# A 128-byte shift of the left-hand tile pools in a one-core decoder trunk

## The chip, the cores and the metric

The kernel runs on one core of a Trainium2 chip. The metric is the time of one execution on the device in microseconds (us). The kernel before took 1058.08 us, the median of three runs.

## The reference

A two-layer decoder trunk over 256 tokens of width 1024, in float32. Each layer is a half-step SwiGLU feed-forward, a token mixer (RWKV-7 time mixing in the first layer, banded attention in the second) and a second half-step feed-forward, each inside a pair of RMS norms. The four feed-forwards hold most of the work:

```python
D_MODEL, SEQ, D_FF = 1024, 256, 2816
def swiglu(x, w_in, w_out):
    gate, up = jnp.split(x @ w_in, 2, axis=-1)
    return (jax.nn.silu(gate) * up) @ w_out

for layer in range(DEPTH):                       # DEPTH = 2
    g = norm_g[layer]
    h = h + 0.5 * rms_norm(swiglu(rms_norm(h, g[0]), ffn_w_in[layer, 0], ffn_w_out[layer, 0]), g[1])
    u = rms_norm(h, g[2])
    m = rwkv7_time_mix(u, ...) if layer < 1 else swa_sinks(u, k_sh, v_sh, ...)
    h = h + rms_norm(m, g[3])
    h = h + 0.5 * rms_norm(swiglu(rms_norm(h, g[4]), ffn_w_in[layer, 1], ffn_w_out[layer, 1]), g[5])
```

After the first layer a shared key and value is projected from the normed residual.

## The kernel before

**Products.** A float32 product is made from float32r halves: each operand is split into a high part (a cast) and the rest (`stream`, L165, for weights; `split`, L313, for activations). `mm3` (L226) then makes three matmuls, high by high, high by low, low by high. The first operand of a matmul is the stationary one, which a weight load (PEld) brings into the array; the second is the moving one, read while the matmul runs.

**Weights.** All weights are streamed in chunks of 128 x 1024 float32 (512 KB). A chunk lands in a staging tile `wr` (L161), ScalarE casts it into the high half of a weight tile (L195), and VectorE subtracts to get the low half (L201). Weight tiles are 8 KB per partition, and come in three pools, `W1`, `W2`, `W3`, in turns:

```python
self.turns = ["W1", "W2", "W2", "W1", "W2", "W2", "W1", "W2"]            # L1483, first feed-forward
self.turns, self.wturn = ["W3"] * 4 + ["W1"] * 3 + ["W2"] * 4, 0         # L1205, the other three and attention
```

The profile leaves out buffer numbers and prints all three as `W`; which pool a chunk lies in follows from counting chunks along `turns`, as the program's allocation does.

**The feed-forward.** `ffn_main` (L449) goes over blocks `b` of 256 hidden features. For each, `feat_pair` (L354) makes the up-projection: the weight is stationary and the normed activations `xt` are moving, in pairs of a 512-column (L362) and a 256-column matmul (L363), 8 pairs for each of the four chunks of `w_in` that a block takes, so 32 pairs a block. Then `down` (L436) makes the down-projection of an earlier block: here the gated activations `g2k` are stationary and the weight is moving, 24 matmuls of 512 columns a block in `mm3` (L227), 12 for each chunk of `w_out`. The last blocks' down-projections run together after the loop (`ffn_tail`, L480; in the third feed-forward `t_end` in the attention region): 72 matmuls in the first feed-forward, 96 in the others. The profile's group `bk<-W,g2k` of L227 is exactly these, 1056 of them, 88 chunks.

Three smaller groups run through L227: the first blocks of each feed-forward, projections of queries, and others with `xt` stationary (`bk<-W,xtl`, `bk<-W,xth`); the shared key and value and the attention's output projection with tiles of pool `ux` stationary (`bk<-W,u`, `bk<-W,xx`); and the time mixer's output projection (`bk<-wo,BK`).

**Where tiles lie.** Each partition's memory is filled by pools from both ends. From the left come the permanent tiles, then `xt`, then a small spacer pool (`sh0`, `sh1` or `sh2`, one for each of the three regions of the program), and then, in the first and third region, the left-hand pools: `W1` (three weight tiles), `g2k` (14 tiles for gated activations and products), `t4` (tiles of 128 x 1024 for norms), and in the third region also `qT`, and `kvp` with the kept key and value. From the right come `ux`, `W2`, `W3` and in the second region the mixer's tiles. Tile sizes in the left-hand pools are multiples of 256 bytes, so that all tiles behind the spacer lie at the same address modulo 256 (their residue below). `xt` begins at residue 0, the spacer is 24 x 4 = 96 bytes, and so `W1`, `g2k`, `t4`, `qT` and `kvp` lie at 96. The right-hand end of the usable memory is at residue 224, and so `W2`, `W3` and `ux` lie at 224. The staging tiles `wr` lie at 64, the identity matrix at 128. Of the second region `sh1` is not touched; most tiles there lie at 224 behind one tile of 8320 bytes, and those of `wo0` and `wo3` at 96.

Order: the program's instructions are put in order by the tile framework, by data and by hand-written lists (`STEPS`, `ATT`) in the second region and the attention. All weight loads are issued by SyncE in one queue.

Of the kernel before, what the change touches and what calls it, by code (L numbers as in the profile page):

```python
# [16 lines left out]
P = 128  # L17
# [60 lines left out]
class Trunk:  # L78
# [508 lines left out]
    def tm_core(self):  # L587
# [35 lines left out]

        acc0, todo = v_half(0, xv)
        run(todo)
        self.mix(xkm[:, :, toks[1]], 2, toks[1])
        self.tm_lora(1)
# [564 lines left out]
        self.close("el1", "Wx", "GR", "GS", "el", "sh1", "xt", "ar")  # L1192
        self.open("xt")
        self.open("sh2")
        self.tl("sh2", [P, 24])
        self.open("g2k", 14)
        self.open("W1", 3)
        self.open("qT")
# [271 lines left out]
    def run(self, out):  # L1470
        nc, a = self.nc, self.a
        self.out = out
        self.tm_open()
        self.open("xt")
        self.open("sh0")
        self.tl("sh0", [P, 24])
        self.open("W1", 3)
        self.open("t4", 4)
        self.open("g2k", 14)
        self.tm_begin()  # L1480
        self.open("l1", side="right")
        self.open("W2", 5, side="right")
        self.turns = ["W1", "W2", "W2", "W1", "W2", "W2", "W1", "W2"]  # L1483

        self.ffn_begin(0, None, 2, 3)
        g_pre = self.gain(R_NORM[(0, 0)])
        self.lead_chunk(0, 0)
        nc.sync.dma_start(self.h[1], a["x"][P:T, :])
        self.xt = xt = self.new_xt("xt")
        for i in range(2):  # L1490
            self.to_xt(i, self.hstat(i), [(g_pre, xt)])
        self.ffn_lead((0, 1))
        self.ffn_main()
        self.load(self.cols, a["cols"], self.mid)
        self.load(self.small, a["small"].to_broadcast([P, 272]), self.mid)
        self.load(self.cst[:, P:], a["consts"][:, P:], self.mid)
        self.tm_consts()
        g_post = self.gain(R_NORM[(0, 1)], self.mid)
        for i in range(2):
            self.tm_in(i, self.post(i, self.ffn_tail(i), g_post, True))  # L1500
        accs, g_post = self.tm_core()

        g_pre = self.gain(R_NORM[(0, 4)])
        xt = self.new_xt("xt")
        for i in range(2):
            self.to_xt(i, self.post(i, accs[i], g_post, False), [(g_pre, xt)])
        self.ffn_begin(1, xt)
        self.plan = list(P1)
        for i in range(2):
            self.ffn_lead((i,))  # L1510
        self.ffn_main()
        g_post = self.gain(R_NORM[(0, 5)], self.mid)

        self.kv_open()
        xt = self.new_xt("xt")
        xe = self.new_xt("ux", ("u", "xx"))
        self.plan = list(PKV)
        self.wkv = [self.stream(a["w_kv"][c], gains=C_GKV + 2 * c) for c in range(3)]
        for i in range(2):
            self.to_xt2(i, self.post(i, self.ffn_tail(i, self.early(i, TX1)), g_post, True), xe, xt)  # L1520
        self.ffn_begin(2, xt, 1)
        for i in range(2):
            self.kv(i, xe)
            self.ffn_lead((i,))
        self.ffn_main()
        self.att_region()
        self.ffn_main()
        g_post = self.gain(R_NORM[(1, 5)], self.mid)
        for i in range(2):
            self.post_last(i, self.ffn_tail(i), g_post)  # L1530
        for p in reversed(self.psum):
            p.release()
        self.close("W3", "W2", "ux", "kvp", "t4", "pad", "qT", "W1", "g2k", "sh2", "xt")
# [88 lines left out]
```

## Time and profile before

| | |
|---|---|
| median of three runs | 1058.08 us (1057.75 to 1059.89) |
| the profiled execution | 1058.52 us, of which the span is 1056.7 us |
| TensorE busy (PE) | 1027.6 us, 97% of the span, 6264 matmuls |
| VectorE busy (DVE) | 699.5 us, 66% |
| ScalarE busy (ACT) | 565.3 us, 53% |
| mean traffic of the memory | 172 GB/s over the span |

The page's first part gives the busy time of each engine, the second the same in 40 slices of the span, the fourth the chain of work that ended last. The time of a single matmul is modelled at its end, and matmuls overlap in the array: the duration of a 512-column matmul reads some 390 ns where the next one begins some 230 ns later. So lengths of whole runs of matmuls are read from the chain in order of time, where pieces stand one behind the other, and the durations serve to compare matmuls of one shape.

### The profile page before, as it was taken

What the parts mean: (1) busy time and instruction counts of PE and PEld (TensorE: products, weight loads), DVE (VectorE), ACT (ScalarE), POOL (GpSimd) and SP (SyncE); (2) the same over time, 40 slices, a digit from 0 to 9 for tenths busy, and PEclk for the clock granted to TensorE, in tenths of its full rate; (3) what the DMA queues carried; (4) which work ended last, traced back from release to release, by engine and by line L of the source; (5) the groups of instructions that cost most, each with busy time, mean ns of one, the idle gap of its engine ahead of it and who ended that gap; (6) DMA issues with size and microseconds to landing.
All of it is one profiled execution on the core that took longest, in us unless ns stands there. A gap on an engine that the chain in (4) does not pass through costs nothing.

```text
span 1056.7 us, 16152 instructions
## 1 busy us (share of the span) xinstructions
PE 1027.6 (97%) x6264; PEld 859.3 (81%) x6264; DVE 699.5 (66%) x1125; ACT 565.3 (53%) x1014; POOL 20.5 (2%) x34
## 2 busy tenths in 40 slices
PE   6999999999999999999999999999999979999997
PEld 5888888779967887888888788888877758888885
DVE  6766655527798977766665676666658876765652
ACT  6654554355244546655455665455556755655541
POOL 0000000000000001000000000000010000000000
PEclk9999999999999999999999999999999999999999
DMA  8868665034354346766563376675535127766621
GB/s 285 248 187 279 220 193 165 23 117 141 120 167 135 122 134 207 258 199 206 194 182 122 116 268 212 209 237 189 180 104 175 41 94 254 237 214 196 183 78 40
DMA packets 52668, 183.04 MB, mean 173 GB/s; under 512 B 5744, under 2 KB 6000, under 8 KB 52464
## 3 DMA queue, kind: packets, MB, share of 16 engines
q1 hardware_dynamic: 52304, 181.49, 53.4%
q8 instruction: 49, 0.80, 0.3%
q10 hardware_dynamic: 288, 0.52, 0.1%
q14 instruction: 27, 0.22, 0.1%
HBM read 180.94 MB, written 1.05 MB: 172 GB/s over the span
## 4 chain that ended last, share of the span: by engine, by line
PE 91%; ACT 3%; DVE 3%; DMA 1%; issue 1%; POOL 0%; SPq 0%; DVEq 0%; POOLq 0%; ACTq 0%
PE bk L227 36%; PE bt L362 13%; PE bk L362 13%; PE bt L363 7%; PE bk L363 7%; PE bk L571 3%; PE bk L617 2%; PE bk L581 1%; PE bt L309 1%; PE bc L1002 1%; PE bk L1053 1%; ACT W L195 1%; PE bk L1397 1%; ACT g2k L1368 1%; DVE t L259 0%
## 5 line engine op out<-in xcount | busy, mean ns | idle before, releaser
L201 DVE TENSOR_TENSOR W<-wr,W 128x1024 fp32r<-128x1024 f32 x280 | 341.2, 1225 | 192.8 <-ACT W L195 191.9
L195 ACT CAST W<-wr 128x1024 fp32r<-128x1024 f32 x280 | 291.8, 1050 | 190.7 <-issue 96.5
L227 PE MATMUL bk<-W,g2k 128*128 128x512 f32 x1056 | 250.7, 394 | 0.0
L227 PEld LDWEIGHTS bk<-W,g2k 128*128 128x128 f32 x1056 | 196.1, 188 | 44.1
L362 PE MATMUL bk<-xtl,W 128*128 128x512 f32 x296 | 104.8, 392 | 0.0
L362 PE MATMUL bt<-xth,W 128*128 128x512 f32 x296 | 104.6, 391 | 0.0
L362 PE MATMUL bt<-xtl,W 128*128 128x512 f32 x296 | 104.4, 391 | 0.0
L362 PE MATMUL bk<-xth,W 128*128 128x512 f32 x296 | 104.4, 391 | 0.0
L363 PE MATMUL bt<-xth,W 128*128 128x256 f32 x296 | 83.3, 281 | 0.0
L363 PE MATMUL bk<-xth,W 128*128 128x256 f32 x296 | 83.2, 281 | 0.0
L363 PE MATMUL bk<-xtl,W 128*128 128x256 f32 x296 | 83.2, 281 | 0.0
L363 PE MATMUL bt<-xtl,W 128*128 128x256 f32 x296 | 83.1, 281 | 0.0
L227 PE MATMUL bk<-W,xtl 128*128 128x512 f32 x216 | 60.4, 427 | 6.4 <-ACT W L195 3.5
L362 PEld LDWEIGHTS bt<-xtl,W 128*128 128x128 f32 x296 | 55.6, 188 | 12.3 <-DVE xtl L350 0.5
L362 PEld LDWEIGHTS bk<-xtl,W 128*128 128x128 f32 x296 | 55.6, 188 | 12.2
L362 PEld LDWEIGHTS bk<-xth,W 128*128 128x128 f32 x296 | 55.6, 188 | 11.9
L362 PEld LDWEIGHTS bt<-xth,W 128*128 128x128 f32 x296 | 55.5, 188 | 11.8
L227 PEld LDWEIGHTS bk<-W,xtl 128*128 128x128 f32 x216 | 42.0, 200 | 20.0 <-ACT W L195 4.0
L363 PEld LDWEIGHTS bk<-xtl,W 128*128 128x128 f32 x296 | 55.9, 189 | 1.4
L363 PEld LDWEIGHTS bt<-xth,W 128*128 128x128 f32 x296 | 55.8, 189 | 0.1
L363 PEld LDWEIGHTS bt<-xtl,W 128*128 128x128 f32 x296 | 55.8, 189 | 0.1
L363 PEld LDWEIGHTS bk<-xth,W 128*128 128x128 f32 x296 | 55.8, 189 | 0.0
(287 smaller groups left out, 1375.7 us busy)
## 6 DMA issues: line engine op xcount, KB each, us to landing
wr<-in_w_in_dram SPq DMA_DIRECT2D x148, 512.0 KB, 3.8
wr<-in_w_out_dram SPq DMA_DIRECT2D x88, 512.0 KB, 3.6
wr<-in_w_in_lead_dram SPq DMA_DIRECT2D x28, 512.0 KB, 4.2
wr<-in_w_v_dram SPq DMA_DIRECT2D x16, 512.0 KB, 3.9
gain<-in_rows_dram SPq DMA_DIRECT2D x13, 512.0 KB, 4.5
wr<-in_w_k_dram SPq DMA_DIRECT2D x8, 512.0 KB, 4.0
wr<-in_w_r_dram SPq DMA_DIRECT2D x8, 512.0 KB, 3.5
wr<-in_w_o_dram SPq DMA_DIRECT2D x8, 512.0 KB, 4.3
```

The lines of the kernel that those rows point to most:

```text
L195: self.follow(nc.scalar.copy(w[:, 0, :], raw), 0)
L201: self.follow(nc.vector.tensor_tensor(w[:, 1, :], raw, w[:, 0, :], op=ALU.subtract), 1)
L227: mm = lambda *x, **y: self.nc.tensor.matmul(*x, **y, **kw)
L309: t = self.nc.tensor.transpose(b[:, k * P:(k + 1) * P], xn[:, c:c + P], self.ident)
L362: mm(banks[j], hi[:, c0:c0 + P], xt[c][:, :, k4, :], start=(k == 0), stop=False)
L363: use[0] = mm(banks[j][:, 0:T], lo[:, c0:c0 + P], xt[c][:, 0, k4, :], start=False, stop=(k == KT - 1))
L571: self.nc.tensor.matmul(b[:, j * T:(j + 1) * T], ws[k // 4][:, c0:c0 + P], xf[:, k, :], start=(k == 0), stop=(k == KT - 1))
L581: nc.tensor.matmul(bs[j], l[:, k, j * P:(j + 1) * P], x[:, k, sl], start=(k == 0 and not e), stop=(k == KT - 1 and e == 1))
L617: mm(acc, x[:, 2 * k2 + k, :], w[:, k, :], start=(k2 + k == 0), stop=(k2 + k == 4))
L1002: mm(b[r, m * N:(m + 1) * N], W[r, v - hh * 16, :], XV[r, v, :], start=True, stop=True)
L1053: mm(out[hh][half[1 - e], m * N:(m + 1) * N], lhs, UV[part][:, hh * 16 + q, :], start=(not i and part == 0 and m == 0), stop=(part == e), ...
L1368: nc.scalar.activation(S[x], S[x], AF.Exp, bias=st[:, 1, x:x + 1], accum_out=st[:, 3, x:x + 1])
```

## The change

Two spacer tiles grow from 24 to 56 float32 numbers, from 96 to 224 bytes:

```diff
@@ tm_core, where the third region opens @@
         self.open("xt")
         self.open("sh2")
-        self.tl("sh2", [P, 24])
+        self.tl("sh2", [P, 56])
         self.open("g2k", 14)
         self.open("W1", 3)
@@ run, where the first region opens @@
         self.open("xt")
         self.open("sh0")
-        self.tl("sh0", [P, 24])
+        self.tl("sh0", [P, 56])
         self.open("W1", 3)
```

Nothing is ever written to or read from a spacer. Every tile behind it on the left moves by 128 bytes. 322 of the program's 1061 tiles move:

| tiles | residue modulo 256 before | after |
|---|---|---|
| `W1`, `g2k`, `t4`, `qT`, `kvp` | 96 | 224 |
| `W2`, `W3`, `ux` | 224 | 224 |
| `xt` | 0 | 0 |
| `wr` | 64 | 64 |
| identity matrix | 128 | 128 |
| second region (`sh1` and what lies behind it) | 96 or 224 | the same |

The instructions of the program, their order on each engine and their waits are the same before and after, row for row, on TensorE, VectorE, ScalarE, GpSimd and SyncE. Only addresses differ.

## Rows read from the trace of the kernel before

**Rows 1.** The page: busy time of three engines, and slices.

```profile
PE 1027.6 (97%) x6264; PEld 859.3 (81%) x6264; DVE 699.5 (66%) x1125; ACT 565.3 (53%) x1014; POOL 20.5 (2%) x34
...
PE   6999999999999999999999999999999979999997
...
PEclk9999999999999999999999999999999999999999
```

**Rows 2.** The page: chain that ended last, share of the span by engine, line.

```profile
PE 91%; ACT 3%; DVE 3%; DMA 1%; issue 1%; POOL 0%; SPq 0%; DVEq 0%; POOLq 0%; ACTq 0%
PE bk L227 36%; PE bt L362 13%; PE bk L362 13%; PE bt L363 7%; PE bk L363 7%; PE bk L571 3%; PE bk L617 2%; PE bk L581 1%; PE bt L309 1%; PE bc L1002 1%; PE bk L1053 1%; ACT W L195 1%; PE bk L1397 1%; ACT g2k L1368 1%; DVE t L259 0%
```

**Rows 3.** Busy time in two stretches, one block long each: start:end, length, engines, clock.

```profile
655.90:672.50 16.60, 16.60 (x90) 14.22 (x89) 10.14 (x16) 8.83 (x14) 0.00 (x0) 1.00 0.63 192
...
705.90:722.50 16.60, 16.60 (x90) 14.28 (x89) 10.13 (x15) 8.82 (x14) 0.00 (x0) 1.00 0.61 189
```

**Rows 4.** Chain in order of time, third feed-forward: start us, us, what, matmuls.

```profile
655.95 5.57 PE bk L227 x24
672.63 5.58 PE bk L227 x24
689.30 5.50 PE bk L227 x24
705.92 5.58 PE bk L227 x24
722.59 5.46 PE bk L227 x24
```

**Rows 5.** Chain in order of time: first feed-forward's blocks and tail; last tail.

```profile
47.99 5.60 PE bk L227 x24
64.72 5.51 PE bk L227 x24
81.35 5.53 PE bk L227 x24
...
181.28 16.05 PE bk L227 x69
...
1027.87 22.26 PE bk L227 x96
```

**Rows 6.** Line L227, all: count, duration ns min/median/max, first and last start.

```profile
L227 PE MATMUL bk<-W,g2k x1056: 387/393/483, 47.8 to 1049.7; 128*128 128x512 f32 x176
...
L227 PE MATMUL bk<-W,xtl x216: 388/396/796, 9.7 to 891.1; 128*128 128x512 f32 x108
...
L227 PE MATMUL bk<-wo,BK x96: 387/389/498, 372.9 to 395.6; 128*128 128x512 f32 x96
...
L227 PE MATMUL bk<-W,u x72: 387/392/504, 586.0 to 848.6; 128*128 128x512 f32 x72
```

**Rows 7.** Line L227 in two stretches, key and value at 588.9, attention output at 828.2.

```profile
L227 PE MATMUL bk<-W,xx x12: 388/389/389, 589.0 to 591.5; 128*128 128x512 f32 x12
...
L227 PE MATMUL bk<-W,xx x12: 392/395/398, 829.7 to 832.3; 128*128 128x512 f32 x12
```

**Rows 8.** Lines L195 and L201, all weight splits: duration ns min/median/max.

```profile
L195 ACT CAST W<-wr x280: 1027/1049/1075, 8.1 to 1019.6; 128x1024 fp32r<-128x1024 f32 x140
...
L201 DVE TENSOR_TENSOR W<-wr,W x280: 1183/1225/1229, 9.2 to 1020.7; 128x1024 fp32r<-128x1024 f32 x140
```

**Rows 9.** Transposes of two lines, matmuls: duration ns min/median/max.

```profile
L806 PE MATMUL bc<-cst,p x16: 272/273/273, 253.6 to 281.3; 128*128 128x128 f32 x16
...
L431 PE MATMUL bk<-cst,g2k x22: 270/272/273, 35.8 to 899.8; 128*128 128x128 f32 x22
```

**Rows 10.** What PE waited for, longest first: us in total, times, longest.

```profile
PE bt L309 <- DVE t L301: 7.7, 1, 7.7
PE bk L227 <- ACT W L195: 3.5, 2, 1.8
PE bk L581 <- ACT u L543: 1.6, 2, 1.4
```

## The prediction

> **What bounds the kernel now.** The page's busy times come first [rows 1]: TensorE is busy 97% of the span, no slice after the first falls under 0.7, and its clock is granted in full throughout, the higher of its two levels, 2.4 GHz. The chain of work that ended last says the same [rows 2]: 91% of it is TensorE's, 36% line L227 alone and 40% the up-projection's lines L362 and L363. TensorE's three longest waits add up to 12.8 us [rows 10]. A stretch of one regular block of a feed-forward, 16.60 us long, has TensorE busy for all of it, VectorE for 10.1 us and ScalarE for 8.8 us, with DMA at 0.6 [rows 3]: the engines that split the weights have 6 us to spare in each block. So here a nanosecond less in a matmul is a nanosecond less in the time, and nothing but matmuls matters much. The change moves no instruction, so the only question is whether a matmul, or what feeds it, takes another time when its operands lie elsewhere.
>
> **What the trace shows of addresses.** The kernel before holds both cases side by side, since W1 lies at residue 96 with g2k, and W2 and W3 at 224. The down-projection of one block is 24 matmuls on two chunks, g2k stationary and W moving. Counted along `turns`, the five blocks of [rows 4] use two W3 chunks (5.57 us), two W2 (5.58), a W3 and a W1 (5.50), two W2 (5.58) and two W1 (5.46). In the first feed-forward two W2 chunks take 5.60 us, one W2 and one W1 5.51 or 5.53 [rows 5]. There the instructions, shapes and surroundings are the same. Where both chunks share the residue of g2k the block takes 0.12 us less than where neither does, and with one of them it lies between: 0.06 us a chunk of 12 matmuls, 5 ns a matmul.
>
> That it is the agreement of the two operands, and not the left side or the number 96, shows where 224 meets 224. `wo` by BK, 72 of 96 with both at 224, has a median of 389 ns, against 393 for W by g2k, of which 74% disagree, and 396 for W by xtl, all of which disagree, with xt at 0 [rows 6]. In the key and value projection W3 moves against xx, both at 224: twelve matmuls between 388 and 389 ns. In the attention's output projection W1, at 96, moves against the same xx: twelve between 392 and 395 at the median, up to 398 [rows 7]. One row speaks less clearly: W by u has 392 ns at the median, though 60 of its 72 agree [rows 6]; they stand at the beginnings of runs, where matmuls still wait for data.
>
> **The change part by part.**
>
> *Down-projections.* 1056 matmuls are 88 chunks. 23 of them lie in W1 and agree already; 65 lie in W2 or W3 and will agree. At 0.06 us each that is 65 x 0.06 = 3.9 us off. In the tails, where W1 chunks alternate with others, they don't reach their 5.46 us a block: the last one takes 22.26 us for 96 matmuls [rows 5] where four blocks of 5.46 would be 21.84, 0.42 less, while its five W2 and W3 chunks alone account for 0.30. This adds 0.1 in each of the two tails that are so mixed, 0.2 in all. From below: if the settled runs of two like chunks are special and only 3 ns a matmul come, 65 x 12 x 3 ns = 2.3 us.
>
> *W1 against u and xx.* 36 matmuls disagree now (96 against 224) and will agree; at 395 against 389 ns [rows 7] that is 0.2 us off.
>
> *W1 against xt.* 168 matmuls go from 96 against 0 to 224 against 0. They disagree before and after, so nothing is taken; up to 0.2 us either way (1 ns each).
>
> *Up-projections.* Here W is stationary and xt, at 0, moves. Between the blocks of [rows 4] stand stretches of 32 pairs: 661.52 to 672.63 is 11.11 us with three W1 chunks and one other, 11.09 with no W1, 11.12 with two, 11.09 with none. W1 costs 0.01 us a chunk at most. If that is its residue, moving its 45 up-projection chunks to 224 gives back 0.4 us; if it is that W1 shares its residue with g2k, which is being written then, all 103 chunks of W2 and W3 will pay it, 1.0 us more. I take 0, between them.
>
> *Splits, norms, transposes.* The casts of weights run from 1027 to 1075 ns with a median of 1049, the subtractions from 1183 to 1229 [rows 8], although 85 of the 280 write to residue 96 and 195 to 224: there are no two levels, and what moves costs nothing. Should they cost 5% more, the 6 us a block that VectorE has to spare hide it. Transposes against the identity at 128 take 272 ns with the tile at 96 (g2k, L431) and 273 with it at 224 (p, L806) [rows 9]: nothing. Scores and values of the attention have both operands in pools that move together.
>
> *Sum.* 3.9 + 0.2 + 0.2 = 4.3 us. These matmuls stand on the chain as whole runs [rows 4, 5], and the weights' loads wait for tiles that TensorE frees, so they begin earlier by as much; of TensorE's 3.5 us of waiting for a weight split [rows 10] a little may grow. I take 0.1 off: 4.2 us. Against the profiled execution's 1058.5 us this gives 1054.3. The median of the runs shown is 0.4 lower; that goes into the range.
>
> **The Trainium skill, weighed against this.** The Trainium skill's page "SBUF — State Buffer" says in its section "SBUF: two separate sides" that within the engines' side only the port pair shared by VectorE and GpSimd contends, and in "A bandwidth-pool intuition that's wrong (but worth ruling out)" that TensorE's weight loads have a read port of their own. By that rule the place of g2k and W can't matter to a matmul, the sum would be 0 and the time 1058.5 us. The trace disagrees by the 0.12 us between like blocks [rows 4], and the measurement decides; the rule's result is the second rival.
>
> **The rivals.**
>
> *Part of the gain.* The agreement helps, but after the change ScalarE and VectorE also write at the residue that TensorE reads, everywhere. Then only the lower 2.3 us come, and the up-projections pay their 1.0: 1058.5 - 1.3 = 1057.2 us. For it: W1's 0.01 us a chunk. Against it: W1 and g2k share a residue already, with g2k written all the time, and that is where the block is shortest.
>
> *No effect.* The 5 ns belong to something that goes with W1, such as its neighbours in time, and not to residues. Then 1058.5 us. Against it stand 224 by 224 at 389 ns and W1 by xx at 395 [rows 6, 7].
>
> *Slower.* In the up-projections W2 and W3, stationary at 224, are loaded while g2k is written; today g2k lies at 96. If the new agreement of writes with weight loads costs these matmuls what disagreement costs the others, 5 ns on each of the 2368 of L362 and L363, that is 11.8 us: 1058.5 - 4.2 + 11.8 = 1066.1 us. From 2.7 ns a matmul (6.3 us) the kernel would be slower by over 0.2%. Against it: the three W1 chunks at 661.52, which agree with g2k today, add 0.02 us in 11.11 us, 0.4 ns for each of their 48 matmuls.
>
> **How the numbers follow.** The forecast has 0.73, between 3.3 and 5.0 us off. Part of the gain has 0.11, no effect 0.10, slower 0.06. A measurement of this kernel can tell about 0.2% (2.1 us) from no change. All of the forecast's case is faster by more, and about a third of the partial one: 0.76. No effect and the rest of the partial case are the same: 0.18. Slower has 0.06. The range goes from 1053.2 (the whole sum with the 0.4 of the up-projections, against the lower median) to 1057.4 (the partial case), which leaves out no effect, slower and a little at the edges.
>
> **What would show it.** Right: the down-projection blocks of 24 matmuls all at 5.45 to 5.48 us on the chain, whichever pool they use; the last tail near 21.9; the median of W by g2k at 389 ns, equal to that of `wo` by BK; up-projection stretches still at 11.09 to 11.12; blocks 16.55 us apart where they are 16.6 to 16.7 now. Wrong: blocks with W2 or W3 still at 5.58 (no effect), or up-projection stretches over 11.2 us (the slower rival), or TensorE waiting longer for splits (L195, L201) by as much as the matmuls gain.

## The result and the profile after

The changed kernel takes 1053.16 us, the median of five runs (1051.64 to 1054.67), against 1058.08 us; the ratio is 0.9949, 95% interval 0.9932 to 0.9967. That is 4.9 us less, where 4.2 were forecast, and the time is 0.04 us under the low end of the forecast's range. The profiled execution is the slowest of the five (1054.67 us): its span is 1052.9 us, 3.8 less than the profiled execution before.

The chain of the changed kernel in order of time (start us, us, what, matmuls), against [rows 4, 5]:

```profile
48.32 5.45 PE bk L227 x24
64.88 5.45 PE bk L227 x24
...
180.85 15.67 PE bk L227 x69
...
653.53 5.45 PE bk L227 x24
670.10 5.45 PE bk L227 x24
686.66 5.45 PE bk L227 x24
703.23 5.45 PE bk L227 x24
719.79 5.45 PE bk L227 x24
...
1024.47 21.79 PE bk L227 x96
```

All regular blocks of W by g2k now take the same time, whatever pool their chunks lie in; in [rows 4], two W2 chunks took 5.58 us, a W3 and a W1 5.50 and two W1 5.46. The first feed-forward's tail went from 16.05 to 15.67 us, the last one's from 22.26 to 21.79. Between the blocks, the up-projection stretches are 11.12, 11.11, 11.12 and 11.11 us long (658.98 to 670.10 and so on), where they were 11.11, 11.09, 11.12 and 11.09; in the first feed-forward the first of them went the other way, from 11.13 us (53.59 to 64.72, [rows 5]) to 11.11 (53.77 to 64.88). The five blocks of [rows 4] began 66.64 us apart from first to last, now 66.26.

Line L227 of the changed kernel, all its matmuls (count, duration ns min/median/max, first and last start, form), against [rows 6]:

```profile
L227 PE MATMUL bk<-W,g2k x1056: 388/389/481, 48.2 to 1045.9; 128*128 128x512 f32 x176
L227 PE MATMUL bk<-W,xtl x216: 392/396/796, 10.1 to 888.4; 128*128 128x512 f32 x108
```

W by g2k has come from 393 to 389 ns at the median, the value that equal residues had elsewhere. W by xtl, whose residues differ before and after, stays at 396. The groups of the two kernels, busy us and mean ns (before first, then after):

```profile
L227 PE MATMUL bk<-W,g2k 128*128 128x512 f32 x1056 | 250.7, 394 | 0.0
```

```profile
L227 PE MATMUL bk<-W,g2k 128*128 128x512 f32 x1056 | 246.0, 390 | 0.0
```

So 4.7 us went out of this one group.

### The profile page after: what moved, and what is told of

It reads as the page before. It is cut to its first block, busy times and chain, and to the rows that moved or that the text cites. A ratio compares the mean times of both kernels' runs of the same rounds, so it can differ in the third digit from the quotient of the medians.

```text
span 1052.9 us, 16152 instructions
## 1 busy us (share of the span) xinstructions
PE 1024.4 (97%) x6264; PEld 860.9 (82%) x6264; DVE 699.4 (66%) x1125; ACT 564.9 (54%) x1014; POOL 20.5 (2%) x34
## 4 chain that ended last, share of the span: by engine, by line
PE 90%; ACT 3%; DVE 3%; DMA 2%; issue 1%; POOL 0%; SPq 0%; DVEq 0%; POOLq 0%; ACTq 0%
PE bk L227 35%; PE bk L362 13%; PE bt L362 13%; PE bt L363 7%; PE bk L363 7%; PE bk L571 3%; PE bk L617 2%; PE bk L581 1%; ACT W L195 1%; DMA wr<-in_w_in_dram 1%; PE bc L1002 1%; PE bk L1053 1%; PE bt L309 1%; DVE W L201 1%; DMA wr<-in_w_in_lead_dram 1%
## 5 line engine op out<-in xcount | busy, mean ns | idle before, releaser
L201 DVE TENSOR_TENSOR W<-wr,W 128x1024 fp32r<-128x1024 f32 x280 | 341.1, 1224 | 190.1 <-ACT W L195 188.7
L195 ACT CAST W<-wr 128x1024 fp32r<-128x1024 f32 x280 | 291.9, 1049 | 189.9 <-issue 94.3
L227 PE MATMUL bk<-W,g2k 128*128 128x512 f32 x1056 | 246.0, 390 | 0.0
L227 PEld LDWEIGHTS bk<-W,g2k 128*128 128x128 f32 x1056 | 195.8, 188 | 40.1
L362 PE MATMUL bk<-xtl,W 128*128 128x512 f32 x296 | 105.1, 393 | 0.0
L362 PE MATMUL bt<-xtl,W 128*128 128x512 f32 x296 | 104.4, 391 | 0.3 <-DVE xtl L350 0.3
L362 PE MATMUL bt<-xth,W 128*128 128x512 f32 x296 | 104.5, 390 | 0.0
L362 PE MATMUL bk<-xth,W 128*128 128x512 f32 x296 | 104.3, 390 | 0.0
L363 PE MATMUL bt<-xth,W 128*128 128x256 f32 x296 | 83.5, 282 | 0.0
L363 PE MATMUL bk<-xth,W 128*128 128x256 f32 x296 | 83.5, 282 | 0.0
L363 PE MATMUL bk<-xtl,W 128*128 128x256 f32 x296 | 83.4, 282 | 0.0
L363 PE MATMUL bt<-xtl,W 128*128 128x256 f32 x296 | 83.4, 282 | 0.0
L227 PE MATMUL bk<-W,xtl 128*128 128x512 f32 x216 | 61.7, 434 | 6.4 <-ACT W L195 3.3
L362 PEld LDWEIGHTS bt<-xtl,W 128*128 128x128 f32 x296 | 55.6, 188 | 12.3 <-DVE xtl L350 0.7
L362 PEld LDWEIGHTS bk<-xtl,W 128*128 128x128 f32 x296 | 55.6, 188 | 12.2
L362 PEld LDWEIGHTS bk<-xth,W 128*128 128x128 f32 x296 | 55.6, 188 | 11.6
L362 PEld LDWEIGHTS bt<-xth,W 128*128 128x128 f32 x296 | 55.5, 188 | 11.6
L227 PEld LDWEIGHTS bk<-W,xtl 128*128 128x128 f32 x216 | 42.9, 204 | 20.3 <-ACT W L195 3.8
L363 PEld LDWEIGHTS bk<-xtl,W 128*128 128x128 f32 x296 | 55.8, 189 | 1.2
L363 PEld LDWEIGHTS bt<-xth,W 128*128 128x128 f32 x296 | 55.9, 189 | 0.1
L363 PEld LDWEIGHTS bt<-xtl,W 128*128 128x128 f32 x296 | 55.9, 189 | 0.1
L363 PEld LDWEIGHTS bk<-xth,W 128*128 128x128 f32 x296 | 55.9, 189 | 0.0
```

Source lines behind the costliest of these rows:

```text
L195: self.follow(nc.scalar.copy(w[:, 0, :], raw), 0)
L201: self.follow(nc.vector.tensor_tensor(w[:, 1, :], raw, w[:, 0, :], op=ALU.subtract), 1)
L227: mm = lambda *x, **y: self.nc.tensor.matmul(*x, **y, **kw)
L362: mm(banks[j], hi[:, c0:c0 + P], xt[c][:, :, k4, :], start=(k == 0), stop=False)
L363: use[0] = mm(banks[j][:, 0:T], lo[:, c0:c0 + P], xt[c][:, 0, k4, :], start=False, stop=(k == KT - 1))
```

## Experiments

**The changed kernel again.** No edit.

> The changed kernel once more. Its first trace has every down-projection block at 5.45 us, W by g2k 4.7 us less busy than before, and up-projection stretches 0.01 us longer at most, so that the matmuls alone account for some 4.5 us. If the residues are the whole of it, the ratio should settle near 0.9957 (4.5 us of 1058). If something else gains too, it should stay at 0.9949 or lower (5.4 us and more), and then a second term is to be found outside lines L227, L362 and L363.

Measured: 1053.3 us (seven runs, 1051.44 to 1056.09), ratio 0.9951 (0.9932 to 0.9970). The interval takes in both 0.9957 and 0.9949, so the time alone doesn't tell whether there is a second term. The traces do. The blocks and tails are those of the first trace to 0.01 us, but this execution's span is 1050.0 us, 2.9 shorter. Of that, 2.7 us lie in one place, the end of the attention, between an output projection and the next feed-forward's first run of 24. Chain rows of before, of the changed kernel's first trace and of its second:

```profile
846.02 4.38 PE bk L227 x18
...
888.68 5.60 PE bk L227 x24
```

```profile
842.50 4.35 PE bk L227 x18
...
886.02 5.59 PE bk L227 x24
```

```profile
842.36 4.35 PE bk L227 x18
...
883.17 5.59 PE bk L227 x24
```

From the first row to the second it is 42.66 us, 43.52 and 40.81. The stretch from 850 to 880 us of the three (length, PE busy and matmuls, granted clock, DMA share, GB/s), in the same order:

```profile
850.00:880.00 30.00, 24.58 (x100) 0.89 0.48 170
```

```profile
850.00:880.00 30.00, 25.29 (x96) 0.83 0.48 170
```

```profile
850.00:880.00 30.00, 25.13 (x111) 0.94 0.52 182
```

TensorE pauses here, in attention's last norms (it is busy for 24.6 to 25.3 of the 30 us), and its clock falls to the lower level, 1.2 GHz, for a part of the stretch that is not the same in two executions of one kernel. The five microseconds from 855 to 860 of the changed kernel's two traces:

```profile
855.00:860.00 5.00, 5.00 (x12) 0.50 0.36 105
```

```profile
855.00:860.00 5.00, 5.00 (x16) 0.70 0.27 105
```

In the first of them the clock is at the lower level throughout, 0.50 of the higher, and 12 matmuls fall into five busy microseconds, in the second 16. Over the whole stretch the mean granted clock is 0.89, 0.83 and 0.94, and the stretch is the longer the lower it is. All eleven traces of this case agree. Where the mean granted clock from 840 to 890 us is 0.97 (four traces), the way from the one chain row to the other takes 40.6 to 41.9 us; at 0.93 (three) it takes 42.3 to 42.7, at 0.90 (four) 43.5 to 43.7. The times of the kernel before sort in the same way: of its 42 runs beside the experiments, the 14 with a mean granted clock of 0.994 or less take 1059.3 to 1062.5 us, the 28 with 0.995 or more 1055.7 to 1058.5.

Outside of this stretch the two traces of the changed kernel agree: up to its beginning they are 3.5 and 3.7 us ahead of before, and behind it both gain another 1.2 us (888.68 to 1027.87 is 139.19 us before, 138.45 and 138.46 after, and the last tail is 0.47 shorter). That is 4.7 and 4.9 us, and the rest of the differences of spans, 3.8 and 6.7, lies in the stretch with the lower clock. The terms that the traces show, 4.7 us off in W by g2k, some 0.15 off in W1 against u and xx less 0.1 by which the up-projections became longer (worked out below), make 4.8, so no second term is needed.

**All at 96.** The left side stays as before, and the right side moves by 128 bytes:

```diff
     def tm_begin(self):
+        self.open("shr", side="right")
+        self.tl("shr", [P, 32])
         self.open("ux", side="right")
```

> The left-hand pools stay at residue 96, and a spacer of 128 bytes on the right moves W2, W3, ux and the mixer's right-hand tiles from 224 to 96, so that weights and gated activations agree at 96 instead of 224. Theory of agreement: all blocks of 24 take 5.45 us as in the changed kernel, median of W by g2k 389 ns, 4 to 5 us off, the same time as the changed kernel within 1 us. Theory of place (224 is a good residue, or tiles on the left must leave 96): blocks stay at 5.5 or get slower, 5.58 and over, and the time is that of before, 1058, or above.

Measured: 1052.73 us (eleven runs), ratio 0.9949 (0.9934 to 0.9965). Chain in order of time, line L227, and the up-projection's two lines, which are read below:

```profile
653.44 5.44 PE bk L227 x24
669.98 5.44 PE bk L227 x24
...
1021.56 21.78 PE bk L227 x96
```

```profile
L227 PE MATMUL bk<-W,g2k x1056: 387/389/477, 48.1 to 1042.9; 128*128 128x512 f32 x176
```

```profile
L362 PE MATMUL bk<-xth,W x296: 391/392/395, 39.3 to 1015.5; 128*128 128x512 f32 x148
```

```profile
L363 PE MATMUL bk<-xth,W x296: 277/280/283, 39.5 to 1015.7; 128*128 128x256 f32 x148
```

The same gain, with nothing on the left moved, and weights, `ux` and g2k all at 96. What counts is that the operands agree; 224 is not special, nor is the left side.

**W1 apart.** g2k moves to 224, W1 stays at 96 by a second spacer, here the third region's:

```diff
-        self.tl("sh2", [P, 24])
+        self.tl("sh2", [P, 56])
         self.open("g2k", 14)
+        self.open("sw2")
+        self.tl("sw2", [P, 32])
         self.open("W1", 3)
```

> g2k moves to 224 as in the changed kernel, but W1 alone (with qT and kvp in the third region) is kept at 96 by a second spacer. Theory of agreement: the pattern of before turns over. Blocks on two W2 or W3 chunks take 5.45 us, blocks on two W1 chunks 5.57 to 5.60, mixed ones 5.50 to 5.53; of the 65 and 23 chunks, 65 gain and 23 lose, so 3.9 - 1.4 = 2.5 us off. A theory that the W1 pool is fast by itself (its neighbours in time) has the W1 blocks stay at 5.46.

Measured: 1055.70 us (twelve runs), ratio 0.9978 (0.9967 to 0.9990), 2.3 us off by the ratio, where 2.5 were expected. Chain in order of time, third feed-forward:

```profile
655.17 5.46 PE bk L227 x24
671.74 5.45 PE bk L227 x24
688.31 5.52 PE bk L227 x24
704.95 5.45 PE bk L227 x24
721.51 5.60 PE bk L227 x24
```

These are the blocks of [rows 4], and the pattern has turned over: two W3 5.46, two W2 5.45, mixed 5.52, two W1 5.60 where they had been the shortest. The no-effect rival, that something else about W1 made its blocks short, has fallen.

**Other distances.** The spacers are set to other lengths, so that W1 and g2k together lie at some other residue while W2 and W3 stay at 224 and xt at 0. Three kernels, two residues each (the three edits are put together, with remarks):

```diff
-        self.tl("sh0", [P, 24])     # and sh2
+        self.tl("sh0", [P, 40])     # 160; sh2 48: 192
+        self.tl("sh0", [P, 16])     # 64;  sh2 32: 128
+        self.tl("sh0", [P, 120])    # 224, 256 bytes further; sh2 64: 0
```

> The left-hand pools (W1 and g2k together) lie at 160 in the first region and at 192 in the third, W2 and W3 at 224, xt at 0. So g2k lies 64 and 32 behind W2 and W3, where it was 128 before. Theory that only equal residues are good: W2 and W3 blocks stay at 5.57 to 5.60, W1 chunks at 2.72 to 2.74, so 5.46 for a block on two W1. Theory of a phase that matters by its size: W2 and W3 blocks lie between 5.45 and 5.58, nearer to 5.45 in the third region (32 apart) than in the first (64 apart). Up-projections on W1, with xt at 0, show what 160 and 192 do there: 348 ns a pair or less if only equality is bad for them.

> The left-hand pools lie at 64 in the first region and at 128 in the third, g2k 160 and 96 behind W2 and W3. Only equal residues good: W2 and W3 blocks at 5.57 to 5.60 in both regions. A phase by its size: blocks slower or faster than 5.58, different in the two regions. Up-projections on W1 show stationary operands at 64 and 128 against xt at 0.

> In the first region the left-hand pools lie at 224 again, but 256 bytes further than in the changed kernel; in the third region they lie at 0, like xt. If the residue modulo 256 is what counts, first-region blocks take 5.45 us as in the changed kernel; if modulo 512, 5.5 or more. In the third region g2k at 0 lies 32 ahead of W2 and W3 at 224: about 5.58 if only equality is good. W1 at 0 equals xt at 0: if equality is what costs the up-projections of the kernel with xt at 224 their 7 ns a pair, the W1 chunks of the third region cost it too, 354 ns a pair against 347, whatever the residue; and W1's matmuls against xt (stationary) become as short as 389 ns.

Measured: 1061.58, 1060.14 and 1056.94 us in one run each, beside 1056.79 for the kernel before. Chain rows of the three in turn: a block on two W2 chunks in the first region, then, in the third, two W3, two W2 and, as the last row, two W1; the rows at 690.52 and 687.71 are blocks on one W3 and one W1, shown because the stretches read below end there:

```profile
48.69 5.51 PE bk L227 x24
...
656.98 5.59 PE bk L227 x24
673.83 5.58 PE bk L227 x24
690.52 5.53 PE bk L227 x24
...
723.89 5.47 PE bk L227 x24
```

```profile
47.19 5.63 PE bk L227 x24
...
655.79 5.61 PE bk L227 x24
672.60 5.61 PE bk L227 x24
...
722.74 5.47 PE bk L227 x24
```

```profile
48.34 5.45 PE bk L227 x24
...
654.15 5.59 PE bk L227 x24
671.00 5.60 PE bk L227 x24
687.71 5.52 PE bk L227 x24
...
721.13 5.45 PE bk L227 x24
```

With g2k behind W2 and W3 by 64 bytes a block takes 5.51 us, by 32 5.58 or 5.59, by 96 5.61, by 160 5.63, and 32 ahead 5.59 or 5.60; 128 apart it was 5.58 [rows 4], or 5.60 in the first feed-forward [rows 5], where 64 and 160 were read. Neither theory came out as it was written. Unequal residues are not all alike, as 5.51 shows, and nearness in itself is no help: 32 is worse than 64. Equal residues are the best of all multiples of 32 that were tried, whichever the residue is: two W1 at 192, 128 and 0 take 5.45 to 5.47. The first region of the third kernel has 256 bytes more between the two sides than the changed kernel, and the same 5.45 us, so that the residue modulo 256 is what counts there.

The up-projections answer in another way. In the third kernel, the stretch from 659.74 to 671.00 us, with three W1 chunks at 0 like xt, is 11.26 us long, and the next one, with W2 and W3 at 224 alone, 11.11 (676.60 to 687.71). In the first kernel, with W1 at 192, the same two are 11.26 and 11.11 us. So here equal residues cost 0.05 us a chunk, and 192 against 0 as much. In the second kernel, with W1 at 128, the first of the two is 11.20 us (661.40 to 672.60), 0.03 us a chunk. Matched with the program's allocation (the matmuls of the trace in order beside those of the program, whose tiles have addresses), the matmuls of W1 with xt standing still, now both at 0 in the third region of the third kernel, did become as short as expected, 389 ns at the median.

The three times can't be put down to one cause. Beside the changed kernel the blocks on W2 and W3 have lost their gain again, up to 0.05 us for each of the 45 up-projection chunks on W1 comes to 2.2 us at most (an estimate), and the clock around 850 us differs: granted 0.90, 0.90 and 0.97 from 840 to 890 us. Each time is a single run.

**xt at 224 too.** The spacer stands ahead of xt:

```diff
+        self.open("shx")
+        self.tl("shx", [P, 56])
         self.open("xt")
-        self.open("sh0")
-        self.tl("sh0", [P, 24])
...
-        self.tl("sh1", [P, 24])
+        self.tl("sh1", [P, 32])
...
-        self.open("sh2")
-        self.tl("sh2", [P, 24])
```

> The spacer of 224 bytes stands ahead of xt instead of behind it, so that xt too lies at 224 with everything of the changed kernel. Theory of agreement: the 432 matmuls of W by xtl and xth (median 396 ns, next one some 234 ns later) come down to 389 (227): 432 x 6 ns = 2.6 us off beyond the changed kernel; the up-projections, where xt moves and W is stationary, may gain up to 1 ns in 228 for the 512-column ones (1.2 us) or nothing; the time mixer's key projection with xt's tiles against wk gains 0 to 0.6 us. 1049.5 to 1051 us. Rival: xt sharing the residue with what ScalarE and VectorE write costs the up-projections, stretches over 11.15 us, and the time is that of the changed kernel or above.

Measured: 1059.83 us (twelve runs), ratio 1.0015 (1.0003 to 1.0028): slower than before, and 6.5 us slower than the changed kernel. Lines L227 and L362, and two blocks of the chain:

```profile
L227 PE MATMUL bk<-W,xtl x216: 387/389/796, 9.5 to 892.7; 128*128 128x512 f32 x108
```

```profile
L362 PE MATMUL bk<-xth,W x296: 391/398/403, 38.5 to 1024.3; 128*128 128x512 f32 x148
```

```profile
657.80 5.50 PE bk L227 x24
674.60 5.50 PE bk L227 x24
```

Both halves of the expectation are borne out, and the cost is the larger. W by xt came down from 396 to 389 ns, as agreement foretold for matmuls of L227. But the 512-column matmuls of the up-projection went from 390 to 398 ns, the stretch between the two blocks is 11.30 us instead of 11.11, and the blocks behind it are 0.05 us longer than in the changed kernel; with 37 blocks that is an estimated 37 x (0.19 + 0.05) = 8.9 us more, against some 2.6 less. The rival's reason, that the operands share a residue with what other engines write, is not borne out: in the changed kernel W shares its residue with g2k, which is written all the time, and L362 stays at 390 ns.

**xt at 128.** One execution: the spacer ahead of xt is 128 bytes, the ones behind it stay at 96, so that W and g2k lie at 224.

> xt moves from 0 to 128, W1, W2, W3 and g2k lie at 224 as in the changed kernel. The weight stands 96 ahead of xt, as it does in the kernel with everything at 96 and xt at 0. If the difference of the two residues is what counts in the up-projections, their medians are 392 ns (L362) and 280 (L363) as there, and not the 390 and 282 of weights at 224 with xt at 0; a pair takes the same 347 ns, and the time is that of the changed kernel, 1052 to 1055. If the place of each operand counts by itself, the medians are others. W by xt, 128 apart no longer equal to 32, stays at 393 ns or more.

Measured: 1056.16 us in one run. Lines L362 and L363, whose matmuls are of 256 columns, first of the changed kernel and then of this one:

```profile
L362 PE MATMUL bk<-xth,W x296: 390/390/397, 39.4 to 1018.4; 128*128 128x512 f32 x148
```

```profile
L363 PE MATMUL bk<-xth,W x296: 278/282/282, 39.6 to 1018.6; 128*128 128x256 f32 x148
```

```profile
L362 PE MATMUL bk<-xth,W x296: 391/392/395, 40.6 to 1019.9; 128*128 128x512 f32 x148
```

```profile
L363 PE MATMUL bk<-xth,W x296: 278/280/281, 40.9 to 1020.2; 128*128 128x256 f32 x148
```

The medians are 392 and 280 ns, those of the kernel with W at 96 and xt at 0, and not the 390 and 282 of W at 224 and xt at 0. Weight and moving operand are 96 apart in both. Equal residues agree with each other too: matched with the allocation, the L362 matmuls on W1 of the third kernel above, at 0 with xt at 0, have the same median of 398 ns as those with both at 224. So in the pairs tried the difference of the two counts, and not the place of either. W by xt stayed at 394 to 396 ns, as expected. The time alone says nothing: it is a single run.

**xt left alone, and its partners moved.** The changed kernel, with weight tiles longer by 256 bytes, so that a chunk can begin 32 bytes further in, at residue 0. The chunks that meet a standing xt do:

```diff
-        w = self.tl(nm, [P, 2, D], F32R)
+        w = self.tl(nm, [P, 2 * D + 64], F32R)[:, at:at + 2 * D].rearrange("p (e c) -> p e c", e=2)
...
-            self.wlead[b, c] = self.stream(self.a["w_in_lead"][self.f, b, c])
+            self.wlead[b, c] = self.stream(self.a["w_in_lead"][self.f, b, c], at=8)
...
-        wq, wo = self.resident(a["w_q"]), self.resident(a["w_ao"])
+        wq, wo = self.resident(a["w_q"], 8), self.resident(a["w_ao"])
```

> The changed kernel, and weight tiles 256 bytes longer, so that a chunk can be laid 32 bytes further in: chunks whose partner is xt standing still (w_in_lead and w_q) are laid at residue 0, like xt, all others stay at 224. For the room, the kept value tile takes the place of a tile of the time mixer (hwa, at residue 0). Theory that L227's matmuls want both operands at one residue: W by xtl and xth, 432 matmuls, come down from a median of 396 ns to 389, some 7 ns each where no wait stands before them, 2 to 2.8 us off the changed kernel, 1050.5 to 1051.3 us; down- and up-projections stay as they are (5.45 us, 11.11 us). Rival: these matmuls stand where TensorE waits for weights anyway, and the time is that of the changed kernel, 1053.

Measured: 1052.10 us (eight runs, 1051.18 to 1056.74), ratio 0.9946 (0.9927 to 0.9966). Line L227:

```profile
L227 PE MATMUL bk<-W,xtl x216: 387/389/796, 10.6 to 885.0; 128*128 128x512 f32 x108
```

The chunk-by-chunk edit, of which the fence shows three places, also puts the kept value tile into `hwa`. The matmuls became as short as expected, 389 ns at the median. The median time is the lowest of all kernels here, but only 1.2 us under the changed kernel's second series, and the intervals overlap almost wholly: that it is faster than the changed kernel is not shown. Between the changed kernel's second trace and this one the span differs by 0.6 us, less than the 2 to 2.8 expected. The two groups of matmuls with xt standing are 2.2 us less busy (W by xtl 58.3 us after 59.2, W by xth 52.6 after 53.9), but part of that goes to the rival: TensorE waits 1.6 us for ScalarE's part of xt (L314) in front of these matmuls, 0.4 in the second trace of the changed kernel.

## Why the prediction came out as it did

The mechanism was right, and so were its place and nearly its size: agreement of the two operands of L227, 5 ns a matmul, on the chain. The step that failed is the size of the first term of the sum, the down-projections, forecast at 4.1 us and measured at 4.7. The range missed by 0.04 us at its low end, which is far less than the scatter of the runs: the second series of the changed kernel, at 1053.30 us, lies inside it. On which side of the bound the first series fell was chance; that the gain was forecast too small was not.

- *Down-projections.* Forecast 3.9 + 0.2 = 4.1 us; measured 4.7 (250.7 to 246.0 us). The prediction charged 5 ns to each disagreeing matmul and took the agreeing ones to be as short as they can be, but for 0.2 us in two tails. Matched one by one with the program's allocation, from one start to the next, the disagreeing matmuls went from 232.9 to 227.5 ns in the mean, 5.4 ns, and the agreeing ones from 228.8 to 227.1. These 1.7 ns for 276 matmuls are 0.5 us that the 5.46 us of a block on two W1 chunks didn't show. Most of it lies in the tails, of which three hold W1 chunks, not two: W1's matmuls stood 231.7 ns apart in the first and 230.0 in the last, and 226.7 after. In the blocks of the first feed-forward a disagreeing chunk cost 0.06 to 0.08 us (5.60 to 5.45 for two, 5.51 and 5.53 to 5.45 for one, [rows 5]). Why agreeing matmuls are longer between disagreeing ones, no run shows.
- *W1 against u and xx.* Forecast 0.2 us; some 0.15, 36 matmuls of 4 ns from one start to the next. The median of W by u went from 392 to 389 ns. The prediction's reading of that row was right: the agreeing matmuls at the beginnings of runs are longer before and after, and 12 of the 72 lie on W1.
- *W1 against xt.* Taken at nothing; on W1 the median is 396 ns before and after.
- *Up-projections.* Taken at 0, the middle between a gain of 0.4 and a loss of 1.0. In the third feed-forward the four stretches together went from 44.41 to 44.46 us, in the first they became shorter; over all stretches of the chain the change is 0.1 us more. The reason given for a loss, writes of g2k at the same residue, is not what the experiments point to: the medians of L362 and L363 follow the distance between W and xt.
- *Splits, norms, transposes.* Nothing was taken, and nothing was seen: casts at 1049 ns and subtractions at 1226 at the median, 1049 and 1225 before.
- *Waits.* The 0.1 taken off for longer waits was not needed; TensorE waited 3.3 us for a weight's cast, 3.5 before.
- *Base and range.* The sum was made against 1058.5 us, the profiled execution, 0.4 over the median. With 4.8 us, as the traces show them, off the median of 1058.1 the sum gives 1053.3. The low end, 1053.2, is 4.9 us under the median; the two terms that the prediction names for it, 4.3 and 0.4, give 1053.4. It left no room for the scatter of the measurement itself: the three runs of before span 2.1 us, and 29 later runs of the same kernel 6.6. The traces show where that comes from, the stretch at 850 us with its lower granted clock, 42.66 us before, 43.52 and 40.81 after. The prediction said that the clock is granted in full throughout, which is a misreading: the row of the page rounds to tenths of 40 slices, and the 0.89 of the stretch didn't show.
- *The rivals.* No effect: fallen, by the kernels at 96 and with W1 apart. With it falls, for this kernel, the reading of the Trainium skill's page "SBUF — State Buffer", section "A bandwidth-pool intuition that's wrong (but worth ruling out)", that a read port of their own for the weight loads makes places indifferent: blocks of 5.45 and 5.58 us differ in nothing but addresses. Part of the gain: fallen. The slower rival didn't come about in the changed kernel, but its place was well chosen: the up-projections can lose 8 ns a 512-column matmul to addresses, when xt agrees with W. Its mechanism, writes of other engines, was not what did it.

What stays open is why the agreement helps one pattern of reads and harms the other. In L227 the moving operand is one run of 512 numbers; in L362 it is two runs of 256 from the high and the low half of xt. No run here shows it. Nor was it tried why the clock's share at 850 us differs.

It is open, too, which stationary tile the moving operand has to agree with, the one in use or the one that is loaded next. Inside a block both lie in one pool, and no experiment parts them. The ends of blocks do, where a tile of the up-projection comes next. Matched with the allocation in the traces of the kernel before and of W1 apart, a last matmul whose own operands agree is followed by the next one after 226 or 227 ns in 18 of 19 cases where the next tile agrees as well, and after 232 to 235 ns in all 11 where it lies 128 away. So the tile loaded next has a part in it. Where the matmul's own operands disagree the ends of blocks give no clear picture (228 to 241 ns).

## What to carry to other kernels

Where TensorE is the bound, look whether the trace holds the same matmul on tiles at two address residues, and compare runs of whole groups, since 5 ns in a matmul that reads 390 are easily taken for scatter. The distance between the two operands modulo 256 bytes is worth setting by spacers, for each pattern of reads apart: what is best for one was among the worst for the other. And before a range is drawn for a gain of half a per cent, the scatter of the runs and any pause in which the clock can fall belong into it.

## What the runs showed of the hardware that was not expected

- The spacing of 512-column float32r matmuls with a new stationary tile each depends on the distance between the tiles of the stationary and the moving operand modulo 256: blocks of 24 between 5.44 us (equal) and 5.63 us (160 apart), 227 to 235 ns a matmul, and not in the order of the distance.
- With a moving operand of two runs of 256 the order is another: 11.11 us a stretch with W 224 ahead of xt, 11.26 with three of four chunks at xt's residue and 11.30 with all.
- The clock of a kernel that keeps TensorE busy for 97% of its span still fell to its lower level in one stretch, around 850 us, in which TensorE pauses. In all eleven traces that stretch is the longer the lower its granted clock is, and between two executions of one kernel it differed by 2.7 us.
